# A row-sum kernel fed by one load queue: one lead load of a row per partition becomes two of one row and of three

## The chip, the cores and the metric

The kernel runs on one core of a Trainium2 chip. Its time is the device time of one execution in microseconds, and a version is judged by the median of several executions. Before the change three of them took 160.58, 160.72 and 160.73 us, so the median is 160.72 us. One further execution was recorded by the hardware profiler; it took 160.62 us, of which 159.3 us is the span from its first to its last recorded event.

## The reference

```python
x = np.random.randn(32, 512, 1024).astype(np.float32)
multiplier = 0.5

def reference(x, multiplier):
    return (np.sum(x, axis=-1) * multiplier).astype(np.float32)
```

The input is 16384 rows of 1024 float32 numbers, 4 KiB a row and 64 MiB in all. Each row gives one number, its sum times 0.5, so the output is 16384 numbers, 64 KiB. Every byte of the input has to be read from HBM once, and there is one addition to each four bytes read.

## The kernel before, in words

The 16384 rows are 128 for each of the 128 SBUF partitions. They come in by loads that SyncE (SP) issues on one queue, which 16 DMA engines serve. The loads are, in the order of the queue:

- the lead: the last 128 rows of the input, one row per partition, into a tile `lead` of its own (line 114);
- blocks 0 to 6, the name `xb` in the profile: 16 rows per partition each, 8 MiB, in three buffers used in turn (line 118). Partition p owns 112 consecutive rows of the input, and a block takes 16 consecutive ones of them, 64 KiB in one piece;
- the tail, 15 rows per partition (`tail`, line 43), read as pieces of 7, 5 and 2 rows (line 157) into the third free buffer, and then the fifteenth row in two parts of 608 and 416 columns into the tile `end` (line 162).

The order is written out by hand; no scheduler moves anything. The first loads that wait for nothing, here the lead and blocks 0 to 2, are moved into the program's entry block (`start_loads_at_entry`, line 203), so that they are issued before the engines meet at the start barrier. Block b from 3 on is issued when VectorE (DVE) has read block b-3, because it goes into the same buffer; `freed` holds the count of the semaphore `dve_done` that says so. The tail's five loads wait for the reading of block 4 (line 156).

DVE sums a whole block with one `reduce_sum` (line 134) and scales the 16 sums of each partition (line 140). For block 6 it takes 8 of the 16 rows, and ScalarE (ACT) takes the other 8, one activation a row with the sum as its second output (`act_row`, line 89). The tail's pieces are shared too: ACT has the rows in `on_act` (line 175), DVE the rest, one row an instruction (`dve_sum`, line 98), which is the custom instruction at line 100 in the profile. The two parts of the last row are added one after the other, the second with the first's sum in front of it (lines 187 and 190).

The lead is summed by DVE before block 0. Its 128 sums stand one in a partition; a 32x32 transpose (line 129) turns them into four rows of 32, so that they are stored as four pieces of 128 B.

Three stores end the queue. The early store (line 167) carries the 112 sums per partition of the blocks, 448 B a piece, and waits for DVE and ACT to be done with block 6. The lead's store follows it (line 171). The last store (line 195) carries the tail's 15 sums per partition, 60 B a piece, and waits for the last instructions of ACT and DVE. SP then waits for all three stores, and the program ends.

Of the kernel before, what the change touches and what calls it, by code (L numbers as in the profile page):

```python
# [9 lines left out]
def kernel(  # L10
# [13 lines left out]
    nc = tc.nc  # L24
# [4 lines left out]
    P = nc.NUM_PARTITIONS  # L29
# [3 lines left out]
    x_flat = x.flatten_outer_dims()  # L33
    N, D = x_flat.shape
    rows = N // P
    out_flat = out.rearrange("b s -> (b s)")
    mul = float(multiplier)

    B = 16
    n_blocks = rows // B  # L40
    assert N == P * rows and rows == n_blocks * B
    own = rows - B
    tail = B - 1
    lead0 = P * (own + tail)
    x_rows = x_flat[0 : P * own, :].rearrange("(p c) d -> p c d", p=P)
    x_last = x_flat[P * own : lead0, :].rearrange("(p c) d -> p c d", p=P)
    x_lead = x_flat[lead0:N, :]
    out_rows = out_flat[0 : P * own].rearrange("(p c) -> p c", p=P)
    out_last = out_flat[P * own : lead0].rearrange("(p c) -> p c", p=P)
    out_lead = out_flat[lead0:N].rearrange("(q c) -> q c", c=32)  # L50

    def sbuf(name, *shape):
        return ctx.enter_context(nc.sbuf_tensor(name, list(shape), fp32)).ap()

    bufs = 3
    buf = [sbuf(f"xb{i}", P, B, D) for i in range(bufs)]
    sums = sbuf("sums", P, rows)
    res = sbuf("res", P, rows)
    cut = 608
    at = 640  # L60
    end = sbuf("end", P, at + D - cut)
    S = 32
    lead = sbuf("lead", P, D)
    lead_sq = sbuf("lead_sq", P, S)
    lead_tr = sbuf("lead_tr", P, S)

    def sem(name):
        return nc.alloc_semaphore(name=name)

    dve_done = sem("dve_done")  # L70
    act_done = sem("act_done")
    counts = {"dve": 0, "act": 0}

    def marks(i, engine):

        s = dve_done if engine == "dve" else act_done
        i.then_inc(s, 1)
        counts[engine] += 1
        return counts[engine]

    def load(name, dst, src, free=None):
        landed = sem(name)
        i = nc.sync.dma_start(out=dst, in_=src)  # L83
        if free is not None:
            i.wait_op(dve_done, free, "sem-ge")
        i.then_inc(landed, 16)
        return landed

    def act_row(t, r, col):
        return nc.scalar.activation(  # L90
            out=t[:, r, :],
            in_=t[:, r, :],
            func=mybir.ActivationFunctionType.Copy,
            scale=mul,
            accum_out=res[:, col : col + 1],
        )

    def dve_sum(row, dst, scale):
        mid = row.shape[-1] // 2
        return nc.vector.tensor_tensor_reduce(  # L100
            out=row[:, 0:mid],
            in0=row[:, 0:mid],
            in1=row[:, mid:],
            scale=scale,
            scalar=0.0,
            op0=ADD,
            op1=ADD,
            accum_out=dst,
        )

    marks(nc.vector.memset(end[:, at - 2 : at], 0.0), "dve")  # L111
    zeroed = marks(nc.vector.memset(lead_sq, 0.0), "dve")  # L112
    freed = []
    lead_landed = load("lead_landed", lead, x_lead)
    for b in range(n_blocks - 1):
        c0 = b * B
        t = buf[b % bufs]
        landed = load(
            f"landed{b}",
            t,  # L120
            x_rows[:, c0 : c0 + B, :],
            freed[b - bufs] if b >= bufs else None,
        )
        h = B if b < n_blocks - 2 else B // 2
        if b == 0:
            nc.vector.wait_ge(lead_landed, 16)
            nc.vector.wait_ge(dve_done, zeroed)
            summed = marks(dve_sum(lead, lead_sq[:, 0:1], mul), "dve")
            turned = nc.vector.transpose(out=lead_tr, in_=lead_sq)  # L129
            turned.wait_op(dve_done, summed, "sem-ge")  # L130
            marks(turned, "dve")
        nc.vector.wait_ge(landed, 16)
        done = marks(
            nc.vector.reduce_sum(  # L134
                out=sums[:, c0 : c0 + h], in_=t[:, 0:h, :], axis=mybir.AxisListType.X
            ),
            "dve",
        )
        freed.append(done)
        scaled = nc.vector.tensor_single_scalar(  # L140
            out=res[:, c0 : c0 + h],
            in_=sums[:, c0 : c0 + h],
            scalar=mul,
            op=mybir.AluOpType.mult,
        )
        scaled.wait_op(dve_done, done, "sem-ge")
        early_dve = marks(scaled, "dve")
        if h < B:
            nc.scalar.wait_ge(landed, 16)
            for r in range(h, B):  # L150
                i = act_row(t, r, c0 + r)
            early_act = marks(i, "act")

    c0 = (n_blocks - 1) * B
    t = buf[(n_blocks - 1) % bufs]
    nc.sync.wait_ge(dve_done, freed[n_blocks - 1 - bufs])
    pieces = [(0, 7), (7, 12), (12, 14)]
    landed = [
        load(f"landed_p{k}", t[:, lo:hi, :], x_last[:, lo:hi, :])
        for k, (lo, hi) in enumerate(pieces)  # L160
    ]
# [6 lines left out]
    early.wait_op(act_done, early_act, "sem-ge")  # L168
    early_stored = sem("early_stored")
    early.then_inc(early_stored, 16)  # L170
    lead_store = nc.sync.dma_start(out=out_lead, in_=lead_tr[0:P:S, :])
    lead_stored = sem("lead_stored")
    lead_store.then_inc(lead_stored, 16)

    on_act = {4, 5, 6, 10, 11, 13}
    for k, (lo, hi) in enumerate(pieces):
        on = [r for r in range(lo, hi) if r in on_act]
        nc.scalar.wait_ge(landed[k], 16)
        for r in on:
            i = act_row(t, r, c0 + r)  # L180
        late_act = marks(i, "act") if k == len(pieces) - 1 else None
        on = [r for r in range(lo, hi) if r not in on_act]
        nc.vector.wait_ge(landed[k], 16)
        for r in on:
            dve_sum(t[:, r, :], res[:, c0 + r : c0 + r + 1], mul)
# [1 line left out]
    first = dve_sum(end[:, 0:cut], end[:, at - 1 : at], 1.0)  # L187

    first.then_inc(landed_end[1], 1)
    final = dve_sum(end[:, at - 2 :], res[:, rows - 2 : rows - 1], mul)  # L190
    final.wait_op(landed_end[1], 17, "sem-ge")
    done = marks(final, "dve")

# [71 lines left out]
```

## Time and profile before

| what | us |
|---|---|
| median of three executions | 160.72 |
| the profiled execution | 160.62 |
| its span | 159.3 |
| DMA engines busy, mean of the 16 | 98.0% of the span |
| DVE busy | 120.2 |
| ACT busy | 16.3 |
| a block of 16 rows, DVE `reduce_sum` | 17.22 |
| a row, ACT activation | 1.04 to 1.06 |
| a row, DVE custom sum | 0.69 |

DVE and ACT busy times are sums over the execution. The DMA figure is the time that packets took on the 16 DMA engines, as a share of 16 spans. "DMA x<-y" in a chain or beside a wait is the wait for the load of x from y to land. A line such as "22.81 17.22 DVE L134 TENSOR_REDUCE ..." of the timeline has the start in us from the start of the span, the length in us, engine, line and operation, and in square brackets how long the engine had been idle and what ended that. SPq is SP's queue: the issuing of a DMA, not its transfer. Matrix and GpSimd engines do no work of this kernel beside four small constants at the start.

### The profile page before, as it was taken

What the parts mean: (1) busy time and instruction counts of PE and PEld (TensorE: products, weight loads), DVE (VectorE), ACT (ScalarE), POOL (GpSimd) and SP (SyncE); (2) the same over time, 40 slices, a digit from 0 to 9 for tenths busy, and PEclk for the clock granted to TensorE, in tenths of its full rate; (3) what the DMA queues carried; (4) which work ended last, traced back from release to release, by engine and by line L of the source; (5) the groups of instructions that cost most, each with busy time, mean ns of one, the idle gap of its engine ahead of it and who ended that gap; (6) DMA issues with size and microseconds to landing.
All of it is one profiled execution on the core that took longest, in us unless ns stands there. A gap on an engine that the chain in (4) does not pass through costs nothing.

```text
span 159.3 us, 128 instructions
## 1 busy us (share of the span) xinstructions
DVE 120.2 (75%) x39; ACT 16.3 (10%) x29; POOL 0.2 (0%) x4
## 2 busy tenths in 40 slices
DVE  2000029999499995999869997899959999599744
ACT  2000000000000000000000000000000000099844
POOL 0000000000000000000000000000000000000000
DMA  9969989899699699699699898996996996999994
GB/s 395 510 280 527 411 379 527 379 411 527 263 527 527 263 527 527 263 527 494 296 527 428 362 527 379 411 527 280 510 527 263 527 527 263 436 403 433 442 397 144
DMA packets 2168, 67.18 MB, mean 422 GB/s; under 512 B 504, under 2 KB 632, under 8 KB 888
## 3 DMA queue, kind: packets, MB, share of 16 engines
q1 hardware_dynamic: 2168, 67.18, 98.0%
HBM read 67.11 MB, written 0.07 MB: 422 GB/s over the span
## 4 chain that ended last, share of the span: by engine, by line
DMA 75%; DVE 22%; SPq 1%; issue 0%
DMA xb<-in_x_dram 52%; DMA end<-in_x_dram 24%; DVE sums L134 22%; SPq L83 1%; DVE end L100 1%; DVE res L140 0%; DVE res L100 0%
## 5 line engine op out<-in xcount | busy, mean ns | idle before, releaser
L134 DVE TENSOR_REDUCE sums<-xb 128x16 f32<-128x16384 f32 (+1 forms) x7 | 112.0, 16001 | 30.3 <-DMA xb<-in_x_dram 30.3
L90 ACT ACTIVATE xb<-xb 128x1024 f32<-128x1024 f32 x14 | 14.6, 1046 | 138.1 <-DMA xb<-in_x_dram 138.0
L100 DVE CUSTOM_DVE_ANT_0 xb<-xb 128x512 f32<-128x512 f32 x8 | 5.1, 689 | 3.9 <-DMA xb<-in_x_dram 3.9
L90 ACT ACTIVATION_READ_ACCUMULATOR xb<-xb 128x1 f32 x14 | 2.6, 188 | 0.0
L111 DVE MEMSET end<- 128x2 f32 x1 | 0.1, 60 | 2.9 <-PEq L26 2.9
L90 ACT ACT_TABLE_LOAD x1 | 1.3, 1283 | 2.9 <-PEq L26 2.9
L140 DVE TENSOR_SCALAR res<-sums 128x16 f32<-128x16 f32 (+1 forms) x7 | 1.2, 174 | 0.2
L100 DVE CUSTOM_DVE_ANT_0 end<-end 128x304 f32<-128x304 f32 (+1 forms) x2 | 0.9, 428 | 0.1
L100 DVE CUSTOM_DVE_ANT_0 lead<-lead 128x512 f32<-128x512 f32 x1 | 0.7, 693 | 0.2 <-DMA lead<-in_x_dram 0.2
L100 DVE DVE_READ_ACCUMULATOR2_ANT res<- 128x1 f32 x9 | 0.8, 83 | 0.0
L129 DVE STREAM_TRANSPOSE lead_tr<-lead_sq 128x32 f32<-128x32 f32 x1 | 0.2, 211 | 0.0
L246 POOL MEMSET const-bfloat16-1.0<- 128x1 bf16 x1 | 0.1, 101 | 0.0
L246 POOL MEMSET const-uint8-127<- 128x1 uint8 x1 | 0.1, 101 | 0.0
L246 POOL MEMSET const-float32-0.0<- 128x1 f32 x1 | 0.1, 98 | 0.2 <-issue 0.2
L246 POOL MEMSET const-float32-1.0<- 128x1 f32 x1 | 0.1, 98 | 0.0
L112 DVE MEMSET lead_sq<- 128x32 f32 x1 | 0.1, 85 | 0.0
L100 DVE DVE_READ_ACCUMULATOR2_ANT end<- 128x1 f32 x1 | 0.1, 84 | 0.0
L100 DVE DVE_READ_ACCUMULATOR2_ANT lead_sq<- 128x1 f32 x1 | 0.1, 83 | 0.0
## 6 DMA issues: line engine op xcount, KB each, us to landing
xb<-in_x_dram SPq DMA_DIRECT2D x1, 3584.0 KB, 29.9
xb<-in_x_dram SPq DMA_DIRECT2D x1, 2560.0 KB, 35.7
xb<-in_x_dram SPq DMA_DIRECT2D x1, 1024.0 KB, 37.7
lead<-in_x_dram SPq DMA_DIRECT2D x1, 512.0 KB, 3.2
end<-in_x_dram SPq DMA_DIRECT2D x1, 304.0 KB, 37.9
end<-in_x_dram SPq DMA_DIRECT2D x1, 208.0 KB, 38.0
xb<-in_x_dram SPq DMA_DIRECT2D x7, 40.8
out_dram<-res SPq DMA_DIRECT2D x1, 56.0 KB, 9.6
```

Source lines behind the costliest of these rows:

```text
L83: i = nc.sync.dma_start(out=dst, in_=src)
L90: return nc.scalar.activation(out=t[:, r, :], in_=t[:, r, :], func=mybir.ActivationFunctionType.Copy, scale=mul, accum_out=res[:, col : co ...
L100: return nc.vector.tensor_tensor_reduce(out=row[:, 0:mid], in0=row[:, 0:mid], in1=row[:, mid:], scale=scale, scalar=0.0, op0=ADD, op1=ADD, ...
L111: marks(nc.vector.memset(end[:, at - 2 : at], 0.0), "dve")
L112: zeroed = marks(nc.vector.memset(lead_sq, 0.0), "dve")
L129: turned = nc.vector.transpose(out=lead_tr, in_=lead_sq)
L134: nc.vector.reduce_sum(out=sums[:, c0 : c0 + h], in_=t[:, 0:h, :], axis=mybir.AxisListType.X),
L140: scaled = nc.vector.tensor_single_scalar(out=res[:, c0 : c0 + h], in_=sums[:, c0 : c0 + h], scalar=mul, op=mybir.AluOpType.mult,)
L246: nc = _bacc.Bacc("TRN2", target_bir_lowering=False, num_devices=1)
```

## The change

The tail loses three rows per partition and has 12 (`tail = B - L` with `L = 4`). The last 512 rows of the input, 2 MiB, are now the lead: four consecutive rows for each partition, so that a partition's part is 16 KiB in one piece of HBM. It is loaded by two loads, the first row of every partition (4 KiB) and then the other three (12 KiB). They land in the third block buffer, `buf[2]`, in place of a tile of their own.

ACT sums the four lead rows, where DVE summed the one. Block 2, which goes into the same buffer, is issued only when ACT has done so; the load therefore waits for something and is no longer moved into the entry block. The entry block still issues four loads: the two leads, block 0 and block 1. The clearing of the transpose tile, the lead's sum and the transpose leave DVE. The four sums of a partition are stored as they stand, 128 pieces of 16 B.

The tail's pieces are 5, 4 and 2 rows where they were 7, 5 and 2, and the last row is split as before. ACT has five of its rows (3, 4, 7, 8, 10) where it had six, DVE six where it had eight, and the last store has 48 B a piece where it had 60.

```diff
-    tail = B - 1
+    L = 4
+    tail = B - L
...
-    x_lead = x_flat[lead0:N, :]
+    x_lead = x_flat[lead0:N, :].rearrange("(p c) d -> p c d", p=P)
...
-    out_lead = out_flat[lead0:N].rearrange("(q c) -> q c", c=32)
+    out_lead = out_flat[lead0:N].rearrange("(p c) -> p c", p=P)
...
-    S = 32
-    lead = sbuf("lead", P, D)
-    lead_sq = sbuf("lead_sq", P, S)
-    lead_tr = sbuf("lead_tr", P, S)
+    lead = buf[2]
+    lead_res = sbuf("lead_res", P, L)
...
-    zeroed = marks(nc.vector.memset(lead_sq, 0.0), "dve")
     freed = []
-    lead_landed = load("lead_landed", lead, x_lead)
+    leads = [(0, 1), (1, L)]
+    lead_landed = [
+        load(f"lead_landed{k}", lead[:, lo:hi, :], x_lead[:, lo:hi, :])
+        for k, (lo, hi) in enumerate(leads)
+    ]
...
-            freed[b - bufs] if b >= bufs else None,
+            freed[b - bufs] if b >= bufs else lead_act if b == 2 else None,
+            act_done if b == 2 else None,
...
-            nc.vector.wait_ge(lead_landed, 16)
-            nc.vector.wait_ge(dve_done, zeroed)
-            summed = marks(dve_sum(lead, lead_sq[:, 0:1], mul), "dve")
-            turned = nc.vector.transpose(out=lead_tr, in_=lead_sq)
-            turned.wait_op(dve_done, summed, "sem-ge")
-            marks(turned, "dve")
+            for k, (lo, hi) in enumerate(leads):
+                nc.scalar.wait_ge(lead_landed[k], 16)
+                for r in range(lo, hi):
+                    i = act_row(lead, r, lead_res[:, r : r + 1])
+            lead_act = marks(i, "act")
...
-    pieces = [(0, 7), (7, 12), (12, 14)]
+    pieces = [(0, 5), (5, 9), (9, 11)]
...
-    lead_store = nc.sync.dma_start(out=out_lead, in_=lead_tr[0:P:S, :])
+    lead_store = nc.sync.dma_start(out=out_lead, in_=lead_res)
+    lead_store.wait_op(act_done, lead_act, "sem-ge")
...
-    on_act = {4, 5, 6, 10, 11, 13}
+    on_act = {3, 4, 7, 8, 10}
```

More of the change, by code (lines that the diff above doesn't have):

```diff
@@ L79, in marks, with load @@
         return counts[engine]
-    def load(name, dst, src, free=None):
+    def load(name, dst, src, free=None, on=None):
         landed = sem(name)
@@ L84, in load, with act_row @@
         if free is not None:
-            i.wait_op(dve_done, free, "sem-ge")
+            i.wait_op(dve_done if on is None else on, free, "sem-ge")
         i.then_inc(landed, 16)
         return landed
-    def act_row(t, r, col):
+    def act_row(t, r, dst):
         return nc.scalar.activation(
@@ L94, in act_row @@
             scale=mul,
-            accum_out=res[:, col : col + 1],
+            accum_out=dst,
         )
@@ L150 @@
             for r in range(h, B):
-                i = act_row(t, r, c0 + r)
+                i = act_row(t, r, res[:, c0 + r : c0 + r + 1])
             early_act = marks(i, "act")
@@ L179 @@
         for r in on:
-            i = act_row(t, r, c0 + r)
+            i = act_row(t, r, res[:, c0 + r : c0 + r + 1])
         late_act = marks(i, "act") if k == len(pieces) - 1 else None
@@ L189 @@
     first.then_inc(landed_end[1], 1)
-    final = dve_sum(end[:, at - 2 :], res[:, rows - 2 : rows - 1], mul)
+    final = dve_sum(end[:, at - 2 :], res[:, own + tail - 1 : own + tail], mul)
     final.wait_op(landed_end[1], 17, "sem-ge")
```

## The prediction

> **What bounds the kernel now.** I read the page's table of busy time first, then the DMA line of the slices, the chain that ended last, and last the timeline, from which all durations come.
>
> ```profile
> DVE 120.2 (75%) x39; ACT 16.3 (10%) x29; POOL 0.2 (0%) x4
> ...
> q1 hardware_dynamic: 2168, 67.18, 98.0%
> ...
> DMA 75%; DVE 22%; SPq 1%; issue 0%
> ```
>
> The 16 DMA engines are busy for 98.0% of the span, and no compute engine is near that. The chain gives DVE 22%, but only because it steps back over two block reads (42.25 and 100.32) to find what freed a buffer. They do not hold the queue up: each new load is issued while one and a half others wait. The chain in order of time shows it, and the timeline gives the beat:
>
> ```profile
> 0.90 41.33 DMA xb<-in_x_dram
> 42.23 0.02 issue
> 42.25 17.23 DVE sums L134
> ...
> 118.91 37.93 DMA end<-in_x_dram
> 156.84 0.02 issue
> 156.87 0.50 DVE end L100 x2
> 157.37 0.02 issue
> 157.39 0.38 DVE end L100
> ```
>
> ```profile
> 3.25 0.69 DVE L100 CUSTOM_DVE_ANT_0 lead<-lead 128x512 f32<-128x512 f32 x1 [0.18 <-DMA lead<-in_x_dram]
> ...
> 22.81 17.22 DVE L134 TENSOR_REDUCE sums<-xb 128x16 f32<-128x16384 f32 x1 [18.62 <-DMA xb<-in_x_dram]
> ...
> 61.61 17.22 DVE L134 TENSOR_REDUCE sums<-xb 128x16 f32<-128x16384 f32 x1 [1.93 <-DMA xb<-in_x_dram]
> ...
> 80.97 17.22 DVE L134 TENSOR_REDUCE sums<-xb 128x16 f32<-128x16384 f32 x1 [1.93 <-DMA xb<-in_x_dram]
> ...
> 139.02 8.69 DVE L134 TENSOR_REDUCE sums<-xb 128x8 f32<-128x8192 f32 x1 [1.93 <-DMA xb<-in_x_dram]
> ...
> 148.00 0.35 SPq L167 DMA_DIRECT2D out_dram<-res  x1
> 148.39 0.62 SPq L171 DMA_DIRECT2D out_dram<-lead_tr  x1
> ...
> 153.63 0.69 DVE L100 CUSTOM_DVE_ANT_0 xb<-xb 128x512 f32<-128x512 f32 x1 [3.28 <-DMA xb<-in_x_dram]
> ...
> 156.12 0.69 DVE L100 CUSTOM_DVE_ANT_0 xb<-xb 128x512 f32<-128x512 f32 x1 [0.57 <-DMA xb<-in_x_dram]
> ...
> 157.80 0.35 SPq L195 DMA_DIRECT2D out_dram<-res  x1
> ```
>
> In each bracket DVE waits for a load, so these starts are landings. Blocks land every 19.36 us (61.61 to 80.97), two rows land in 2.49 us (153.63 to 156.12). With F for a load whatever its length and R for a row of all partitions, F + 16R = 19.36 and F + 2R = 2.49, hence R = 1.205 us and F = 0.08 us. A check: block 6 at 139.02, and then pieces of 7 and 5 rows, give 139.02 + 8.52 + 6.11 = 153.65, where 153.63 is seen. The end is the queue's end plus the last store, and the price of any change to the loads is in F and R.
>
> **The loads.** Rows: three more per partition in the leads, three fewer in the tail, 128 in all as before, so 3R - 3R = 0. Loads: 13 before, 14 after, so +F = 0.08 us, all of it on the queue that sets the end. Blocks are unchanged. The second lead's 12 KiB packets are new, but 8 and 20 KiB ones are in this trace (the pieces of 2 and 5 rows), and F and R fit both. From the second lead on every landing moves by F + 3R = 3.70 us, and the tail takes 3R less from block 6 to its end.
>
> Here a rule speaks against the change. The Trainium skill, page "DMA: Bandwidth & Descriptors", section "Anatomy of one DMA — SWDGE (gpsimd) path", fits a transfer as about 2.0 us fixed plus its bytes over 436 GB/s; were the fixed part paid in the queue for one load more, the sum would be 162.6 us. The trace has 0.08 for it, since the next load's packets run while the last one's completion is on its way; the sum goes by 0.08.
>
> **The start.** The entry block issues four loads as before. The second lead takes the place of block 0 in the queue and needs no more issue time (0.39 to 0.46 us each, against 1.285 us for the first lead's data). The new address step is the unknown: partition rows lie 16 KiB apart in HBM, where the lead's were contiguous. Nearest rows: block 0 landed 19.56 us after the lead, 0.20 over the beat; and by the trace's packet records the lead's 128 packets took 0.159 us in the median, 0.187 in the mean and 0.58 at worst, which is 8 x 0.028 = 0.22 us lost per engine. So 0.42 us of start losses are in the 160.62. Bounds: all of them gone, -0.42, or the 1.17-fold stretch (0.187 over 0.159) of the lead also over the second lead, 0.17 x 3.70 = +0.63. I take 0, since blocks that step 448 KiB from partition to partition keep 8.39 MB in 19.36 us, and so do the tail pieces at 60 KiB.
>
> **ACT and the new wait.** DVE loses a memset, a sum and a transpose at 3 to 4.2 us, inside its idle 18.6 us before block 0: worth 0. ACT's table load ends at 4.15; its first lead row follows, the other three from the second lead's landing at 3.25 + 3.70 = 6.95. Eight rows take it 8.42 us (139.02 to 147.44), so three end near 10.2. Block 2's load is then issued near 10.7 instead of by 1.8. Two blocks are queued ahead of it, and the second lands at 42.25 + 3.70 = 45.95, so 35 us cover it. If that cover were gone, the queue would run dry for the whole delay. Behind block 2's load on SP stands block 3's, which waits for DVE's reading of block 0, at 40.06 + 3.70 = 43.76; nothing else is held up. That load comes 2.2 us before block 1 lands, as before, with all of block 2 still queued. The tail's loads follow block 4, at about 121.3, while block 5 is arriving and block 6 is queued. All worth 0.
>
> **The tail's compute.** Block 6 lands at 142.72. DVE takes 8.80 us until its first tail sum (139.02 to 147.82), so it is free at 151.52, ACT at 151.14. Piece 0 (5 rows) lands at 142.72 + 0.08 + 6.03 = 148.83 and waits. DVE's three sums, 0.61 us apart and 0.69 for the last, end at 153.43; ACT's two rows (2.19 us, as at 153.63 to 155.82) near 153.35. Piece 1 lands at 148.83 + 0.08 + 4.82 = 153.73, with 0.30 us to spare. Its two sums and two activations end at 155.03 and 155.92, before piece 2 at 156.22, 0.1 later than now. From there one row on each engine and the two parts of the last row are as they were. Were the 0.30 gone, the two sums of piece 1 would start late, and 1.2 us still lie before piece 2. Worth 0.
>
> **The stores.** DVE's scaling of block 6 moves 3.70 us, so the early store is issued at 151.7 instead of 148.00 and the lead's is through SP by 152.8. Both still stand behind the last loads in the queue: the early store landed 9.6 us after its issue, at 157.6, which is behind the end loads. The lead store's 128 pieces of 16 B are not in this trace. By the final store's 128 pieces of 60 B (packets of 8 to 11 ns, eight per engine) they take 0.09 us; if they held the queue for that store's whole 1.4 us from issue to landing, they would be done at 159.0, and the final store, issued at 157.8, would wait up to 1.2 us. Nothing speaks for a gain: 0 to +1.2. I take 0, by the packets: 0.09 us from 157.6 is over before the final store's own first packets, at 158.65 in the records. That store's smaller pieces (48 B for 60) are worth 0.
>
> **Sum.** 160.62 + 0.08 = 160.70 us. The profiled execution is 0.10 us under the median of the three, which themselves span 0.15.
>
> **The rivals.**
> - Slower, by the start: the 16 KiB step keeps the second lead at the lead's starting pace. For it: the lead's worst packets and the 0.20 of block 0. Against it: the full rate of blocks at 448 KiB and of the tail. It gives between 0.20 and 0.63 more, say 161.15, and decides from 0.34 on. The Trainium skill, same page, section "Latency and other measured facts", has HBM rows a large power of two apart (512 KiB and up) running slower, down to half; no run here shows 16 KiB doing so.
> - Faster, by the start: the 3.70 us of small packets let the engines fall out of step, so block 0 finds them settled, and the engine that came last in the lead is no longer 0.5 us behind the first (its landing counts ran from 2.71 to 3.22, and block 6's still from 138.50 to 138.99). For it: block 0's 0.20 is lost once, and later blocks keep the beat. Against it: the first lead starts as before. Nearly all of the 0.42 would have to go, for 160.30.
> - Slower, by the stores: half of their bound, 161.30. For it: so small a piece is not in the trace. Against: the packet times and the 1 us of idle queue before the final store's packets.
> - Slower, by a fixed cost: the load more is paid as a load alone would be. The lead took 3.2 us from issue to landing, 1.285 of it data, so 1.9 us: 162.5. For it: that a load alone costs this. Against it: in the tail five loads follow each other and piece 1 and piece 2 are within 0.02 us of F and R. It stands for the page's rule above.
>
> That the change does nothing it says, with the same queue and the same bytes, is the forecast itself.
>
> **How the numbers follow.** 0.2% (0.32 us, 160.40 to 161.04) is about what a measurement of this kernel can tell from no change. Forecast 0.57; slower by the start 0.21; by the stores 0.06; by a fixed cost 0.02; faster by the start 0.14. So faster 0.14, same 0.57, slower 0.29. The time is the forecast's, 160.70, whose own range is 160.45 to 161.00. To leave out no more than 2 in 10 the range reaches to the start's two rivals and the stores' half bound, 160.30 to 161.30; only the fixed cost and the far ends of the others stay outside.
>
> **What would show it.** The second lead's landing (ACT's second lead row) 3.70 us after the first's, and block 0's 19.36 to 19.56 us after that; blocks at 19.36 us; piece 2 near 156.2; the final store's issue near 157.9 and 1.4 us to landing; the lead store landing before it. Wrong would be a second lead of 3.9 us or more, block 0 at less than the beat, a DVE or ACT wait in the tail that no DMA ends, or a last store of over 1.5 us.

## The result, and the profile after

The changed kernel takes 161.93 us, the median of six executions from 161.77 to 162.00. The kernel before, measured beside it, takes 160.59 us (160.56 to 160.73). The ratio is 1.008 with a 95% interval of 1.0067 to 1.0093, so the change costs 1.34 us. The forecast was 160.70, in a range that ended at 161.30. The profiled execution took 161.94 us with a span of 160.6; before, these were 160.62 and 159.3.

The page of the changed kernel, busy times and DMA queue and chain:

```profile
DVE 118.0 (73%) x31; ACT 19.5 (12%) x35; POOL 0.2 (0%) x4
...
q1 hardware_dynamic: 2448, 67.18, 97.5%
...
DMA 75%; DVE 22%; SPq 1%; issue 0%
```

Nothing here has another shape than before. The queue still carries the kernel, DVE lost the lead's work and two rows of the tail, ACT has three rows more. The loss is a shift in time, and the timeline shows where it begins:

```profile
4.58 1.06 ACT L89 ACTIVATE xb<-xb 128x1024 f32<-128x1024 f32 x1 [0.37 <-DMA xb<-in_x_dram]
...
8.29 1.06 ACT L89 ACTIVATE xb<-xb 128x1024 f32<-128x1024 f32 x1 [2.56 <-DMA xb<-in_x_dram]
...
27.65 17.22 DVE L136 TENSOR_REDUCE sums<-xb 128x16 f32<-128x16384 f32 x1 [24.60 <-DMA xb<-in_x_dram]
...
66.35 17.22 DVE L136 TENSOR_REDUCE sums<-xb 128x16 f32<-128x16384 f32 x1 [1.93 <-DMA xb<-in_x_dram]
...
85.70 17.22 DVE L136 TENSOR_REDUCE sums<-xb 128x16 f32<-128x16384 f32 x1 [1.92 <-DMA xb<-in_x_dram]
...
143.75 8.69 DVE L136 TENSOR_REDUCE sums<-xb 128x8 f32<-128x8192 f32 x1 [1.92 <-DMA xb<-in_x_dram]
...
154.74 0.69 DVE L99 CUSTOM_DVE_ANT_0 xb<-xb 128x512 f32<-128x512 f32 x1 [0.27 <-DMA xb<-in_x_dram]
...
157.25 0.69 DVE L99 CUSTOM_DVE_ANT_0 xb<-xb 128x512 f32<-128x512 f32 x1 [1.20 <-DMA xb<-in_x_dram]
...
158.97 0.33 SPq L198 DMA_DIRECT2D out_dram<-res  x1
```

The first lead is there at 4.58 us, where before it was there at 3.25: 1.33 us late, on the same 512 KiB. The second lead follows 3.71 us later and block 0 another 19.36. Blocks keep their beat (66.35 to 85.70), the tail's last piece starts at 157.25 instead of 156.12, and the last store is issued at 158.97 instead of 157.80, 1.17 us later. The shift stands at the first landing already, 1.33 us of it, and 1.17 us of it are left at the last store's issue.

The windows of the first microseconds give the other side of it (columns: length of the stretch, DVE, ACT and POOL busy with their instructions, clock, DMA share, GB/s; a packet counts in the stretch in which it starts, so shares above 1 occur). Before:

```profile
0.00:2.00 2.00, 0.00 (x0) 0.00 (x0) 0.20 (x4) 1.00 0.48 156
2.00:4.00 2.00, 0.84 (x5) 1.13 (x1) 0.00 (x0) 1.00 1.55 631
```

After:

```profile
0.00:2.00 2.00, 0.00 (x0) 0.00 (x0) 0.20 (x4) 1.00 0.42 115
2.00:4.00 2.00, 0.06 (x1) 1.08 (x1) 0.00 (x0) 1.00 0.90 283
```

In the first 2 us the engines are almost as busy as before (0.42 for 0.48) and move a quarter less (115 GB/s for 156): each packet takes longer. The packet records say the same. The 128 packets of 4 KiB took 0.248 us in the mean, up to 0.91, where they took 0.187, up to 0.58.

The trace also has the counts that a load's semaphore receives, one from each of the 16 DMA engines. For the first lead they came between 2.71 and 3.22 us before, and between 3.37 and 4.55 after. I call the distance of the last from the first the spread: 0.51 and 1.19 us. It lasts. Block 6's counts are 0.49 apart before (138.50 to 138.99) and 1.18 after (142.54 to 143.73). A load's 128 packets are eight for an engine on average. A load has landed when its last engine is done: ACT starts at 4.58, behind the last count at 4.55. But the loss is not the slowest engine's alone. The mean of the 16 counts of the first lead moves from 2.95 to 3.86 us, by 0.91 of the 1.33; by the other 0.42 the last engine is farther behind the mean.

The last store took 1.61 us from its issue to its last count (158.97 to 160.58), 1.44 before (157.80 to 159.24). So 1.17 of the loss is in the loads and 0.17 in that store.

### The profile page after: what moved, and what is told of

It is laid out like the page before. It is cut to its first block, busy times and chain, and to the rows that moved or that the text cites. A ratio compares the mean times of both kernels' runs of the same rounds, so it can differ in the third digit from the quotient of the medians.

```text
span 160.6 us, 126 instructions
## 1 busy us (share of the span) xinstructions
DVE 118.0 (73%) x31; ACT 19.5 (12%) x35; POOL 0.2 (0%) x4
## 4 chain that ended last, share of the span: by engine, by line
DMA 75%; DVE 22%; SPq 1%; issue 0%
DMA xb<-in_x_dram 54%; DVE sums L136 21%; DMA end<-in_x_dram 21%; SPq L82 1%; DVE end L99 1%; DVE res L142 0%; DVE res L99 0%
## 5 line engine op out<-in xcount | busy, mean ns | idle before, releaser
L89 ACT ACTIVATE xb<-xb 128x1024 f32<-128x1024 f32 x17 | 17.8, 1046 | 136.0 <-DMA xb<-in_x_dram 136.0
L99 DVE CUSTOM_DVE_ANT_0 xb<-xb 128x512 f32<-128x512 f32 x6 | 3.9, 688 | 1.5 <-DMA xb<-in_x_dram 1.5
L89 ACT ACTIVATION_READ_ACCUMULATOR xb<-xb 128x1 f32 x17 | 3.2, 188 | 0.0
```

What stands on the lines that cost most here:

```text
L89: return nc.scalar.activation(out=t[:, r, :], in_=t[:, r, :], func=mybir.ActivationFunctionType.Copy, scale=mul, accum_out=dst,)
L99: return nc.vector.tensor_tensor_reduce(out=row[:, 0:mid], in0=row[:, 0:mid], in1=row[:, mid:], scale=scale, scalar=0.0, op0=ADD, op1=ADD, ...
```

## The experiments

Theory A came from the views above: the first lead's 128 rows lie 16 KiB apart instead of one behind the other, that slows its packets and spreads the engines, and nothing later closes the spread. Theory B was anything else in the new start: the block buffer as target, a second lead behind the first, block 2 out of the entry. The store had theories of its own. All runs are collected here; "first landing" is the last count of the kernel's first load, with the spread behind it, "last store" is issue to last count in the profiled execution. Landings and stores come from one profiled execution of each kernel. How far such figures scatter is seen on b_store48 and b_pat, which start just as the kernel before does: first landings at 3.40 and 3.34 us where it has 3.22, spreads of 0.37 and 0.52 where it has 0.51.

| kernel | median us | beside it, before | ratio, 95% interval | first landing, spread | last store |
|---|---|---|---|---|---|
| before | 160.59 | | | 3.22, 0.51 | 1.44 |
| changed | 161.93 | 160.59 | 1.0067 to 1.0093 | 4.55, 1.19 | 1.61 |
| b_step2: before, lead rows 8 KiB apart | 161.82 | 160.56 | 1.0062 to 1.0092 | 4.54, 1.22 | 1.43 |
| b_step3: 12 KiB apart | 160.67 | 160.64 | 0.9990 to 1.0009 | 3.66, 0.58 | 1.42 |
| b_step4: 16 KiB apart | 161.62 | 160.61 | 1.0052 to 1.0082 | 4.51, 1.17 | 1.42 |
| b_step5: 20 KiB apart | 160.84 | 160.61 | 1.0006 to 1.0024 | 3.84, 0.72 | 1.42 |
| b_nolead: before, no lead | 160.80 | 160.56 | 1.0003 to 1.0022 | 21.95, 0.53 | 1.41 |
| a_contig: changed, leads contiguous | 160.88 | 160.61 | 1.0006 to 1.0025 | 3.31, 0.39 | 1.54 |
| a_mix: changed, only the first lead contiguous | 161.72 | 160.64 | 1.0045 to 1.0075 | 3.49, 0.42 | 1.77 |
| a_one: changed, one lead of 16 KiB packets | 161.43 | 160.56 | 1.0036 to 1.0066 | 7.72, 0.69 | 1.74 |
| a_L3: changed, three lead rows | 161.01 | 160.59 | 1.0017 to 1.0039 | 3.57, 0.42 | 1.54 |
| a_nostore: changed, lead not stored | 162.22 | 160.61 | 1.0088 to 1.0122 | 4.62, 1.13 | 1.93 |
| a_ns60: the same, last store 60 B pieces | 161.92 | 160.64 | 1.0059 to 1.0089 | 4.59, 1.11 | 1.55 |
| b_store48: before, last store 48 B pieces | 160.58 | 160.56 | 0.9990 to 1.0009 | 3.40, 0.37 | 1.41 |
| b_pat: before, both store patterns | 161.08 | 160.65 | 1.0017 to 1.0045 | 3.34, 0.52 | 1.78 |

### The step alone, on the kernel before

```diff
-    x_lead = x_flat[lead0:N, :]
+    x_lead = x_flat[N - P * 4 : N, :].rearrange("(p c) d -> p c d", p=P)[:, 0, :]
```

> The kernel before, with one edit: the lead's 128 rows are read 16 KiB apart (every fourth of the last 512 rows) and not contiguously. Same bytes, packets, tiles and stores; the sums of the last 128 outputs are of other rows. Theory A (the address step of the first lead slows its packets and spreads the engines, and the spread lasts): the lead's last landing moves from 3.2 to about 4.5 us, its spread over the engines from 0.5 to about 1.2 us, block 0 follows it by 19.36 instead of 19.57, and the time is 161.5 to 161.8. Theory B (something else in the new start: the block buffer as target, the second lead behind the first, block 2 out of the entry): the lead lands at 3.2 and the time stays at 160.6.

Its timeline:

```profile
4.53 0.69 DVE L100 CUSTOM_DVE_ANT_0 lead<-lead 128x512 f32<-128x512 f32 x1 [1.39 <-DMA lead<-in_x_dram]
...
23.94 17.22 DVE L134 TENSOR_REDUCE sums<-xb 128x16 f32<-128x16384 f32 x1 [18.46 <-DMA xb<-in_x_dram]
...
158.82 0.34 SPq L195 DMA_DIRECT2D out_dram<-res  x1
```

One address step, and nothing else of the change, brings the lead from 3.25 to 4.53 us and the time from 160.61 to 161.62. Block 0 comes 19.41 us later, where it came 19.57 us after the lead before; but that difference is within the scatter, since in b_store48 and b_pat, whose start is that of the kernel before, it came 19.37 and 19.40 us after. The spread is 1.17 us at the lead and 0.95 from block 0 on, so a little of it was closed. Theory A has the start; B alone cannot.

### The step taken out of the changed kernel

```diff
-    x_lead = x_flat[lead0:N, :].rearrange("(p c) d -> p c d", p=P)
+    x_lead1 = x_flat[lead0 : lead0 + P, :].rearrange("(p c) d -> p c d", p=P)
+    x_lead3 = x_flat[lead0 + P : N, :].rearrange("(p c) d -> p c d", p=P)
...
-        load(f"lead_landed{k}", lead[:, lo:hi, :], x_lead[:, lo:hi, :])
+        load(f"lead_landed{k}", lead[:, lo:hi, :], (x_lead1, x_lead3)[k])
```

> The changed kernel, with the first lead reading 128 contiguous rows and the second 12 KiB per partition from the 384 contiguous rows behind them; targets, packets, waits and stores unchanged, so that the sums of the last 512 rows are stored in another order. Theory A: the first lead's last landing goes back to about 3.2 us, the time to 160.7 to 160.9, of which 0.17 is the slower last store. Theory B: the first lead still lands near 4.5 and the time stays at 161.9.

```profile
4.15 1.06 ACT L90 ACTIVATE xb<-xb 128x1024 f32<-128x1024 f32 x1
...
6.99 1.06 ACT L90 ACTIVATE xb<-xb 128x1024 f32<-128x1024 f32 x1 [1.69 <-DMA xb<-in_x_dram]
...
26.48 17.22 DVE L137 TENSOR_REDUCE sums<-xb 128x16 f32<-128x16384 f32 x1 [23.49 <-DMA xb<-in_x_dram]
...
157.88 0.33 SPq L199 DMA_DIRECT2D out_dram<-res  x1
```

ACT's first lead row has no wait in brackets: the row landed at 3.31 us and waited for ACT's table load. The last store is issued at 157.88, where before it was 157.80. The 0.08 between them is what F allows for one load more; single profiles don't prove it, since three kernels of the frame before with a quick lead (b_step3, b_store48, b_pat) issue it between 157.70 and 157.92. But two leads, ACT on the lead, the buffer shared with block 2, the new wait and the shorter tail are worth no more than about that. What else the profiled execution (160.79) has above 160.61 is the last store, 1.54 us for 1.44.

### Which steps hurt

The same edit with every second, third and fifth row.

```diff
-    x_lead = x_flat[lead0:N, :]
+    x_lead = x_flat[N - P * 2 : N, :].rearrange("(p c) d -> p c d", p=P)[:, 0, :]
```

> The kernel before, with the lead's 128 rows 8 KiB apart (every second of the last 256). So far: contiguous lands at 3.22 us, 20 KiB at 3.84, 16 KiB at 4.51. If the power of two in the step is what hurts, 8 KiB lies between contiguous and 16 KiB: last landing 3.5 to 4.2, time 160.8 to 161.3. If rows that don't follow each other cost the same at any step, it is as 20 KiB, 3.8, and 16 KiB is the exception: 160.8 to 160.9. If the span of addresses counts, less than 20 KiB: under 3.6 and 160.7.

> The kernel before with the lead's rows 12 KiB apart (every third of the last 384). The lead landed at 3.2 us for 4 KiB, 4.54 for 8, 4.51 for 16, 3.84 for 20. If an even number of rows in the step is what hurts, 12 KiB is as 20 or better: 3.2 to 3.9, spread 0.5 to 0.8, time 160.6 to 160.9. If any gap up to 16 KiB hurts as much, 4.5 and 161.6 to 161.8.

> The kernel before, with the lead's 128 rows read 20 KiB apart (every fifth of the last 640 rows). Theory A1 (a step of a power of two puts the engines in lock step on the same part of HBM): 20 KiB is as good as contiguous, the lead lands near 3.2 us, time 160.6. Theory A2 (rows that are not contiguous are slow whatever the step): the lead lands at 4.5 us or later, time 161.5 to 161.8. Theory B: no change, 160.6.

The lead's landing, from the three timelines, 8 KiB first:

```profile
4.56 0.69 DVE L100 CUSTOM_DVE_ANT_0 lead<-lead 128x512 f32<-128x512 f32 x1 [1.11 <-DMA lead<-in_x_dram]
```

12 KiB:

```profile
3.68 0.69 DVE L100 CUSTOM_DVE_ANT_0 lead<-lead 128x512 f32<-128x512 f32 x1 [0.62 <-DMA lead<-in_x_dram]
```

20 KiB:

```profile
3.86 0.69 DVE L100 CUSTOM_DVE_ANT_0 lead<-lead 128x512 f32<-128x512 f32 x1 [0.66 <-DMA lead<-in_x_dram]
```

Neither the gap nor the span of addresses orders them, since 8 KiB is far worse than 12 and 20. Steps of one, three and five rows land at 3.2 to 3.9 us, steps of two and four at 4.5. My guess that 8 KiB lies between contiguous and 16 KiB was wrong: it is no better than 16. For 20 KiB I expected a landing at 3.2 or at 4.5, and 3.84 is neither. The 12 KiB step costs no time that this measurement shows, the 20 KiB one 0.23 us. Why, of these five steps, the even ones cost so much, no run here shows.

### Only the first packets, or whenever the engines are in step

The first lead reads contiguous rows; the second is the changed kernel's own, 12 KiB packets 16 KiB apart. The bytes are the same, but 128 rows are read twice and 128 not at all.

```diff
-        load(f"lead_landed{k}", lead[:, lo:hi, :], x_lead[:, lo:hi, :])
+        load(
+            f"lead_landed{k}",
+            lead[:, lo:hi, :],
+            x_flat[lead0 : lead0 + P, :].rearrange("(p c) d -> p c d", p=P)
+            if k == 0
+            else x_lead[:, lo:hi, :],
+        )
```

> The changed kernel with the first lead reading 128 contiguous rows, as in the run with both leads contiguous, but the second lead left as it is, 12 KiB packets 16 KiB apart (128 rows are read twice and 128 not at all; the bytes are the same). The first lead should land at 3.3 us with a spread of 0.4. If the step hurts whenever the engines are still in step, the second lead spreads them to about 1 us and lands 4.2 or more after the first: time 161.4 to 161.8. If only the first packets of the program suffer from it, the second lead lands 3.65 to 3.75 after the first and the time is 160.8 to 161.0.

```profile
4.15 1.06 ACT L89 ACTIVATE xb<-xb 128x1024 f32<-128x1024 f32 x1
...
7.80 1.06 ACT L89 ACTIVATE xb<-xb 128x1024 f32<-128x1024 f32 x1 [2.49 <-DMA xb<-in_x_dram]
...
27.36 17.22 DVE L142 TENSOR_REDUCE sums<-xb 128x16 f32<-128x16384 f32 x1 [24.38 <-DMA xb<-in_x_dram]
```

The first lead lands at 3.49 with a spread of 0.42, and then the second takes 4.29 us (to 7.78), its packets 0.536 us in the mean. In the changed kernel the same load, with the same addresses, took 3.71 us and 0.463 a packet. So the step also hurts a load whose packets are not the program's first. The time, 161.72, is that of the first branch.

The spread is not that of the first branch. It is 0.54 us after the second lead and 0.67 from block 0 on, where about 1 was expected. Most of the loss is common to the engines: the mean of block 6's 16 counts is 143.02 us, as late as the changed kernel's 143.01, where it is 142.31 in a_contig. By the last of these counts (143.44, 143.72 and 142.56) the changed kernel is 0.28 us behind a_mix, and that is its wider spread.

Why the changed kernel's second lead loses nothing is argued, not shown. Its engines enter it 1.19 us apart, those of a_mix 0.42, and that would fit engines that hinder each other when they run nearly together. But the two runs also differ in the rows that the first lead has just read, and no run changes the spread alone.

### Larger packets, and no lead at all

One lead of four rows leaves no gaps in HBM: 16 KiB packets that follow each other, 16 KiB from partition to partition.

```diff
-    leads = [(0, 1), (1, L)]
+    leads = [(0, L)]
```

> The changed kernel with one lead of four rows per partition, 16 KiB packets that follow each other in HBM, in place of leads of 4 and 12 KiB. One load fewer is -0.08. If the step between partitions alone does it, the spread is 1.1 to 1.2 us and the time 161.7 to 161.9; if it takes gaps between the packets, the lead lands with a spread of 0.5, block 0 follows at 19.4 to 19.6, and the time is 160.6 to 160.9 with the slower last store in it.

The 2 MiB land at 7.72 us, where the two contiguous leads landed at 6.97 in spite of a load more. The spread is 0.69 and the time 161.43, between the two expectations. Closing the gaps does not mend it; what this kernel has in common with the changed one and with b_step4 is the distance between partitions.

Without any lead, the first load is block 0, 64 KiB packets 448 KiB apart, and the tail has 16 rows.

```diff
-    tail = B - 1
+    tail = B
...
-    lead_landed = load("lead_landed", lead, x_lead)
...
-            summed = marks(dve_sum(lead, lead_sq[:, 0:1], mul), "dve")
...
-    pieces = [(0, 7), (7, 12), (12, 14)]
+    pieces = [(0, 8), (8, 13), (13, 15)]
...
-    lead_store = nc.sync.dma_start(out=out_lead, in_=lead_tr[0:P:S, :])
...
-    on_act = {4, 5, 6, 10, 11, 13}
+    on_act = {4, 5, 6, 7, 11, 12, 14}
```

> The kernel before without a lead: the tail has 16 rows (pieces of 8, 5 and 2, the last row in two parts), block 0 is the first load, stepping 448 KiB from partition to partition, and the last store has 64 B a piece. One load fewer is -0.08. If a first load whose partitions lie a multiple of 16 KiB apart spreads the engines, as the 16 KiB lead did, block 0's landings spread over 1 us or more and the time is 161.0 to 161.6. If it is the small packets at such a step, and not the step, the spread stays at 0.5 and the time is 160.3 to 160.6.

The spread stayed at 0.53, but the time did not fall: 160.80 against 160.56. The packet records show a loss at the start: the first 16 packets of 64 KiB took from 2.60 to 3.37 us, where the median is 2.418. So this step cost every engine something and spread none, and both expectations failed. Summed over the queue, the 64 KiB packets took 14.8 ns more in the mean than in the median, which is 0.83 us over an engine's 56 of them, where in the kernel before the lead's 0.22 and the blocks' 0.35 (6.3 ns on 56) make 0.58. That sum does not settle the time, since by it b_store48 lost 0.81 us, at 160.58. What is measured is that the kernel before is 0.2 us quicker with its small contiguous lead than without one.

### An odd step in the changed kernel

Three lead rows are 12 KiB from partition to partition. The tail has 13 rows in pieces of 6, 4 and 2, and everything is computed.

```diff
-    L = 4
+    L = 3
...
-    pieces = [(0, 5), (5, 9), (9, 11)]
+    pieces = [(0, 6), (6, 10), (10, 12)]
...
-    on_act = {3, 4, 7, 8, 10}
+    on_act = {3, 4, 5, 8, 9, 11}
```

> The changed kernel with three lead rows per partition for four (leads of 4 and 8 KiB packets, 12 KiB from partition to partition), 13 tail rows in pieces of 6, 4 and 2 and the last one, 12 B and 52 B pieces in the stores. Everything is computed. If the parity of the step is what cost the time, both leads run as at 12 KiB: the first lands at 3.3 to 3.7 us with a spread of 0.4 to 0.6, the second 2.45 to 2.6 after it, and the time is 160.7 to 161.0, with up to 0.2 of it from the stores. If two leads of partition pieces are slow at any step, the first lands at 4.5 and the time is 161.6 to 162.0.

The first lead landed at 3.57 us with a spread of 0.42, the second 2.66 us after it, and the time is 161.01; the last two lie just outside of what was expected. It takes back 0.9 of the 1.34 us, with a step of 12 KiB instead of 16. It still does not beat the kernel before, and no version here does: the last store is issued at 158.12, 0.32 later than before, and takes 0.1 longer.

### The last store

```diff
-    lead_store = nc.sync.dma_start(out=out_lead, in_=lead_res)
-    lead_store.wait_op(act_done, lead_act, "sem-ge")
-    lead_stored = sem("lead_stored")
-    lead_store.then_inc(lead_stored, 16)
...
-    nc.sync.wait_ge(lead_stored, 16)
```

> The changed kernel without the store of the lead sums (the last 512 outputs are not written). In the changed kernel the last store takes 1.61 us from issue to landing, before it took 1.44. Theory S16 (the 16 B pieces ahead of it slow the last store's writes): 1.44 again, and the time falls by 0.15 to 0.2 us to about 161.75. Theory S48 (its own pieces of 48 B for 60 B, or the wider spread of the engines, are slower): 1.6 stays and the time with it, 161.9.

This went the wrong way. Without the 16 B store ahead of it the last store took 1.93 us (159.01 to 160.94), not 1.44, and the kernel was 0.29 us slower than with it. So I tried the 48 B pieces alone on the kernel before, by cutting its last store from 15 columns to 12:

```diff
-    out_last = out_flat[P * own : lead0].rearrange("(p c) -> p c", p=P)
+    out_last = out_flat[P * own : P * (own + 12)].rearrange("(p c) -> p c", p=P)
...
-    store = nc.sync.dma_start(out=out_last, in_=res[:, own : own + tail])
+    store = nc.sync.dma_start(out=out_last, in_=res[:, own + 3 : own + tail])
```

> The kernel before, with the last store cut to 12 of its 15 columns, 48 B a piece for 60 (three of the tail's rows are not stored, and the others go to other places). In the changed kernel the last store took 1.61 us, without the 16 B store before it 1.93, and here 1.44. Theory S48 (pieces of 48 B are the slower ones): 1.6 to 1.9, time 160.75 to 161.1. Theory S16 is down, since the store got slower without the 16 B pieces. Theory spread (the engines' wider spread makes it slow): 1.44 and 160.6.

They took 1.41 us, and the time did not move (160.58 against 160.56). The wider spread is not the cause either: with spreads of 1.22 and 1.17 us at the lead, b_step2 and b_step4 have last stores of 1.43 and 1.42. On the changed kernel without the lead's store, 60 B pieces at the addresses of the kernel before:

```diff
-    out_last = out_flat[P * own : lead0].rearrange("(p c) -> p c", p=P)
+    out_last = out_flat[P * own : P * (own + 15)].rearrange("(p c) -> p c", p=P)
...
-    store = nc.sync.dma_start(out=out_last, in_=res[:, own : own + tail])
+    store = nc.sync.dma_start(out=out_last, in_=res[:, own - 3 : own + tail])
```

> The changed kernel without the lead's store, as before in the run without it, and with the last store 15 columns wide, 60 B a piece at the addresses that the kernel before writes (three columns of the early sums are written again, and no store carries the lead's). Without the lead's store the last store of 48 B took 1.93 us. If it is the 48 B pieces together with what only the changed kernel has, it is back at 1.4 to 1.45 and the time at 161.7 to 161.8. If the pieces' size is not the cause, it stays at 1.6 to 1.9 and the time near 162.2.

1.55 us, between the two answers; the time fell from 162.22 to 161.92, with a queue that ended at the same place. Last, both patterns of the changed kernel, 16 B and 48 B, in the frame of the kernel before:

```diff
-    out_last = out_flat[P * own : lead0].rearrange("(p c) -> p c", p=P)
-    out_lead = out_flat[lead0:N].rearrange("(q c) -> q c", c=32)
+    out_last = out_flat[P * own : P * (own + 12)].rearrange("(p c) -> p c", p=P)
+    out_lead = out_flat[P * (own + 12) : N].rearrange("(p c) -> p c", p=P)
...
-    lead_store = nc.sync.dma_start(out=out_lead, in_=lead_tr[0:P:S, :])
+    lead_store = nc.sync.dma_start(out=out_lead, in_=lead_sq[:, 0:4])
...
-    store = nc.sync.dma_start(out=out_last, in_=res[:, own : own + tail])
+    store = nc.sync.dma_start(out=out_last, in_=res[:, own + 3 : own + tail])
```

> The kernel before with the store patterns of the changed one: 128 pieces of 16 B in place of the lead's four of 128 B, and a last store of 48 B pieces at the changed kernel's addresses (only one of each four lead values is a sum, and three of the tail's columns are not stored). Last stores so far, from issue to landing: 1.44 us before, 1.41 with 48 B pieces alone, 1.61 in the changed kernel, 1.93 in it without the lead's store, 1.55 in it with 60 B pieces and no lead's store. If the patterns together make the store slow, 1.5 to 1.7 here and the early store lands later than 157.8; time 160.7 to 160.9. If they do not, 1.4 to 1.45 and 160.6, and the cause lies in the rest of the changed kernel.

Its DMA issues (size of each, us from issue to landing):

```profile
out_dram<-res SPq DMA_DIRECT2D x1, 56.0 KB, 10.4
out_dram<-lead_sq SPq DMA_DIRECT2D x1, 2.0 KB, 10.1
out_dram<-res SPq DMA_DIRECT2D x1, 6.0 KB, 1.8
```

With 48 B pieces but the lead's four pieces of 128 B:

```profile
out_dram<-res SPq DMA_DIRECT2D x1, 56.0 KB, 9.6
out_dram<-lead_tr SPq DMA_DIRECT2D x1, 0.5 KB
out_dram<-res SPq DMA_DIRECT2D x1, 6.0 KB, 1.4
```

Where 128 pieces of 16 B stand ahead of it, the last store takes 1.78 us instead of 1.41, the early store beside them lands 0.8 us later after its issue, and the time is 161.08 against 160.65; store and time are somewhat more than was expected. The packets are not slower: the 16 B ones took 9 ns each, and the last store's first packet came 0.83 us after the issue, as in the kernels before (0.85) and changed (0.83). The counts come late, from two to four of the engines. So the 16 B pieces cost something in this frame, after the packets and before the counts.

The early store shows the same in every kernel. Its last count came 0.38 to 1.28 us behind that of the last load in the six kernels with a store of 128 pieces of 16 B (12 B in a_L3) behind it, and 0.20 to 0.26 behind it in the nine that do not.

That does not explain the changed kernel without them, whose last store with 48 B pieces was slower still, 1.93 us. There too counts came late, from three engines (160.50, 160.63 and 160.94 us, the others by 160.37), with no 16 B piece ahead. Something else in the changed frame must be at work in it, and I have not found it. How the 0.17 us divides between the 16 B pieces and that is open; the store's time in single profiles runs from 1.54 to 1.93 in all kernels of the changed frame and from 1.41 to 1.44 in all of the frame before but the last one tried.

## Why the prediction was wrong

**The start** is the step that failed. It saw the unknown, rows 16 KiB apart, and set it to 0 because blocks at 448 KiB and tail pieces at 60 KiB run at the full rate. But neither is the first load of a program, and neither has the lead's 4 KiB packets or a step of 16 KiB; the only load in that trace that met the start was the lead, and it was contiguous. Its rows were not near to the case in the thing that mattered, a step at the start. The measured term is +1.33 us at the first lead's last landing, -0.21 at block 0 (19.36 instead of 19.57 us), and +0.04 for the rest of the queue: 1.17 at its end. The -0.21 can't be put down to the step. Block 0 landed between 22.73 and 22.79 us in the three kernels with the start of the kernel before, and only the lead's own landing scattered, from 3.22 to 3.40.

Which difference protects the blocks, the runs do not separate. It is not the spread by itself: b_store48's engines are 0.37 us apart when block 0 comes at its 448 KiB step, and it takes 19.37 us, the beat; a_mix's are 0.42 apart when the second lead comes at 16 KiB, and it takes 0.59 too long. Step, packet size and place in the queue all differ between these two.

**The bounds** of that step failed too. It ran to +0.63 by stretching the second lead at the first lead's pace, and took the first lead itself as unchanged. It was the other way round: the second lead took 3.71 us, where 3.70 was forecast, and the first was the slow one. The rival "slower, by the start" had the right cause, the step, with 0.21 for a chance; but it too put the loss into the second lead, and its price, 0.45 us, is less than half of the 1.17. The signs of being wrong were counted from the first landing (second lead, block 0), so they could not show a late first lead; only piece 2, at 157.25 for 156.2, and the last store's issue, at 158.97 for 157.9, showed it. The Trainium skill, page "DMA: Bandwidth & Descriptors", section "Latency and other measured facts", puts slow row pitches at large powers of two, from 512 KiB up; here 8 and 16 KiB were enough, on 4 KiB rows at the start, and the 448 KiB of the blocks cost nothing that shows after block 0.

**The rival "faster, by the start"** took block 0's 0.20 above the beat for a loss of engines in step. With the same start b_store48 and b_pat have 19.37 and 19.40 us there, so most of it was scatter. And a wider spread is no gain, because the last engine ends the queue.

**The loads.** F and R held as far as the scatter lets one see: in the changed kernel the rest of the queue is 0.04 us longer, where 0.08 was forecast, and its 12 KiB packets took 0.460 us in the median, where 8 and 20 KiB ones before had taken 0.311 and 0.761. The fixed-cost rival of 1.9 us is refuted. So are the 2.0 us that the Trainium skill's fit (same page, "Anatomy of one DMA — SWDGE (gpsimd) path"), made for transfers issued by GpSimd and not by SP, would add if the fixed part were paid in the queue.

**ACT and the new wait.** ACT's lead rows ended at 11.5 us instead of 10.2, because the leads were late, and block 2's load went out behind them. Block 1 landed at 46.97, so the cover was 35 us, as forecast. Worth 0.

**The tail's compute.** Block 6 landed 1.03 us later than forecast and all of the tail with it. DVE waited 0.27 us for piece 1 and ACT 0.48, where 0.30 and 0.38 to spare were forecast. Worth 0.

**The stores.** Taken as 0 with a bound of 1.2, measured at 0.17. The packets were as cheap as forecast, and the last store did not wait behind the 16 B pieces (its first packet came 0.83 us after its issue, 0.85 before). The completion was slower, and the sum had no term for it.

## What to carry to other kernels

A start has its own prices. A rate read from the middle of a stream says nothing on the first load: look there at the distance in HBM from partition to partition, and of the steps tried here prefer contiguous rows, or 12 KiB, to 8 or 16 KiB. In a kernel bound by one queue, read the counts of a load's 16 engines and not only the landing, since what the engines, and above all the slowest, lose in the first microseconds is still missing at the end.

## What the runs showed of the hardware that was not expected

- The first load's 4 KiB packets took 0.187 us in the mean at a step of 4 KiB, 0.242 at 8, 0.234 at 12, 0.255 at 16 and 0.238 at 20. These means are close from 8 KiB up. The landings are not: the last count came at 3.22, 4.54, 3.66, 4.51 and 3.84 us, the mean of the 16 counts at 2.95, 3.80, 3.31, 3.81 and 3.45, and the times are 160.6, 161.8, 160.7, 161.6 and 160.8. So at 8 and 16 KiB two thirds of the loss are the average engine's, and one third is the spread.
- From block 1 to the tail's pieces the spread of the counts changes by less than 0.15 us in every kernel run, whether it is 0.4 or 1.2 us, over some 110 us and 48 MiB. Ahead of block 1 it can change: from 1.17 to 0.95 in b_step4, from 0.42 to 0.67 in a_mix.
- 128 pieces of 16 B held up the counts of stores, though their packets took 9 ns each: in b_pat the early store landed 10.4 us after issue, 9.6 without them in b_store48, and the last one 1.78 us after, for 1.41.
